# Ordering GpSimd's operator work by VectorE's reads, and next states ahead of the GELU's transposes, in the S5 stages of a hybrid trunk

## The chip, the cores and the metric

The kernel runs on one core of one Trainium2 chip. The metric is the device time of one execution in microseconds. Three runs of the kernel before took 2251.64, 2251.73 and 2249.75 us, the median is 2251.64 us. The core has TensorE (PE in the profile, with its weight loads as PEld), VectorE (DVE), ScalarE (ACT), GpSimd (POOL) and SyncE (SP, which here only issues transfers).

## The reference

The model is a trunk of four layers over a sequence of 512 rows and 1024 columns in float32. The mixers are S5, gated linear attention, differential attention, and S5 again; each is followed by a SwiGLU network with 2816 hidden columns. The change lies in the two S5 mixers. Cut to what matters, one of them computes:

```python
ab = exp(lam * dt)                      # complex, 64 groups x 64 states
bb = (ab - 1) / lam * b                 # 64 groups x 64 states x 16 inputs
u  = rmsnorm(x, g)                      # 512 x (64 groups x 16 inputs)
s[t] = ab * s[t-1] + bb @ u[t]          # per group: a complex scan over time
y[t] = real(c @ s[t]) + d * u[t]
z  = gelu(y)
a, b = split(z @ w_glu, 2)              # 1024 x 2048
x  = x + a * sigmoid(b)
```

## The kernel before, in words

**Tiling.** The 64 groups are worked in eight rounds kk of eight groups, four pairs of two groups b in each; a pair's two times 64 complex states fill the 128 partitions. Time is folded: 512 rows are 128 steps m of four rows each, so that a state advances by the fourth power of ab per step. For each round there are small operators: `in` (two 128x512 tiles, from X), `out` (from Q), `map` (the direct path of the four rows onto one another, from X, Q and d), `cs` (cosine and sine of the phase at each m) and `r4` (the decay per step).

**The pipe.** `s5_pipe` does both S5 stages. Its parts for round kk are:

- `up_first`, `up`: TensorE transposes the input of the round (`up` tile), ScalarE (in the second S5's first four rounds VectorE) copies it to `room`.
- `products` (L1588): 8 TensorE products of `room` with `in` into the two PSUM banks `V`.
- `states` (L1593 to L1598): six VectorE operations 128x512; the first four read `V` from PSUM and `cs`, the last two add in SBUF. The results are in `mods` (m[:, 0] and m[:, 2]; m[:, 2] is written last).
- `scan` (L1602): two VectorE scans over m, both inputs in SBUF.
- `turn` (L1611, L1615): four VectorE products that turn the states back into `prods` (q), both inputs in SBUF.
- `outputs` (L1622, L1624): for each pair b one TensorE product of `room` with `map` and four of `prods` with `out`, all into the PSUM tile `y`; then ScalarE's GELU (L1626).
- `turned` (L1642, L1643): four TensorE transposes of the GELU's output into the PSUM tile `zp`, and ScalarE's rounded copy of it into `zT`; `rest` (L1647): VectorE's remainder of the rounding, the second half of `zT`.
- `glu`: twelve TensorE products per round (L448 to L450) of `zT` with the rounded weights and their remainder into four accumulators. Each product comes in three parts: high by high, high by low, low by high.

The tiles `up`, `xps`, `y`, `zp`, `rps` and `cps` share two PSUM banks (tag "tp"); `rough`, `angle` and the GLU's accumulators share four (tag "acc").

**The order of the work.** Within the pipe the order on every engine and queue is the order in which the code issues it (`hand_all`): nothing is moved by the planner there. Ahead of the pipe, `hand` fixes TensorE's and ScalarE's order only, and behind the pipe the planner of the framework orders the work by its own costs. In round kk the loop issues the states of kk, the outputs of kk-1, the transposes `up` of kk+2, `turned(kk-1)`, `products(kk+1)`, the scans and turns of kk, `rest(kk-1)` and `glu(kk-2)`. Hooks put a stage's own work between these.

**The first S5's own work.** `s5_first` makes the operators inside the pipe, for groups of two rounds h = 0 to 3. `s5_x` makes X[h] in three parts: `pre` (the gain's product L1264, then six operations of 128 columns, L1239 to L1241), `one` and `two` (three operations of 384 columns each). h = 0 is VectorE's, the others are GpSimd's. `s5_q` makes Q[h] on VectorE (six operations of 512 columns in the odd rounds), from a product and a ScalarE copy in the even round before. `ins` transposes X on TensorE (`xps`) and ScalarE copies it into `in` (L1409). `rows` multiplies X's and Q's first parts (`rps`, L1352), and `s5_map` combines them on VectorE and ScalarE, writes them to DRAM (`rd`, L1368, SP's queue) and reads them back as `map` by four transfers on SP's queue and four on GpSimd's (L1377). The phases are made by `rough` and `angle` products on TensorE out of `counts` and `frow`, with ScalarE's roundings, VectorE's `clip` (L1212, a PSUM read) and ScalarE's sines. Tables for the sine and the GELU are loaded anew by ScalarE when it goes from one to the other (1.28 us each).

Before the change, `new_x(1)` is issued ahead of the pipe and runs on GpSimd from 22.4 us; `new_x(2)` and `new_x(3)` are issued whole behind the turns of rounds 1 and 3. No semaphore other than the data's own holds them back.

**The second S5** reads its operators from DRAM, where the first layer's network has spilled them; it has no operator work in the pipe.

## Time and profile before

| what | us |
|---|---|
| median of three runs | 2251.64 |
| the profiled execution | 2249.67 |
| its span | 2248.0 |
| TensorE busy | 2174.6 (97%) |
| VectorE busy | 1635.6 (73%) |
| ScalarE busy | 1138.7 (51%) |
| GpSimd busy | 341.1 (15%) |
| first S5's states, round 0 to round 7 | 31.2 to 125.6 |
| second S5's states, round 0 to round 7 | 1746.9 to 1815.8 |

A row of the timeline has the start, the length, the engine, the line of the kernel, the operation, what it writes and reads, the shape, and how many it merges; in brackets stands how long the engine was idle before and who released it. A row of the waits has the engine, the waiting tile and line, the releaser, the total, the times and the longest. A row of the chain has start, length, engine, tile and line. A row of a source line has the shortest, the median and the longest duration in ns. The end of a VectorE operation overlaps the start of the next by some 0.08 us, so operations of 0.68 us stand 0.60 us apart.

### The profile page before, as it was taken

To read this page: it belongs to the slowest core of one execution; us is meant where nothing else is said; L and a number is where in the kernel's file an instruction comes from. 1 tells how busy PE (TensorE), PEld (TensorE's weight loads), DVE (VectorE), ACT (ScalarE), POOL (GpSimd) and SP (SyncE) were. 2 spreads that over 40 slices of the span, in tenths; PEclk is the share of its full clock that TensorE was granted. 3 is DMA by queue.
4 is the path that set the end of the run, shared out by engine and by line. 5 is a ranking of instruction groups with operands and counts; after the bars stand their busy time and mean duration, and the time that the engine had idled before them with its cause. 6 is when DMAs were issued, how large, how long until landed. Compare 5 with 4: busy or idle time off the path is not lost.

```text
span 2248.0 us, 38450 instructions
## 1 busy us (share of the span) xinstructions
PE 2174.6 (97%) x15415; PEld 1971.6 (88%) x15415; DVE 1635.6 (73%) x2495; ACT 1138.7 (51%) x1827; POOL 341.1 (15%) x447
## 2 busy tenths in 40 slices
PE   6999999999999999999999999999999899999998
PEld 5888979989988899999888888999998888989997
DVE  9955868786878598776745676967766965957675
ACT  8534635444655365564435776644544234635443
POOL 5401141431211010100002221110000001101000
PEclk9999999999999999999999999999999999999999
DMA  4356666674863666765337465985631546766622
GB/s 90 65 171 169 164 159 174 174 184 131 206 152 95 168 168 191 179 171 139 104 128 160 96 148 141 243 207 136 184 94 47 160 141 159 196 160 164 165 76 75
DMA packets 309180, 333.62 MB, mean 148 GB/s; under 512 B 70477, under 2 KB 253033, under 8 KB 308874
## 3 DMA queue, kind: packets, MB, share of 16 engines
q1 hardware_dynamic: 238970, 238.93, 35.0%
q0 software_dynamic: 70032, 92.23, 21.9%
q8 instruction: 121, 1.98, 0.4%
q14 instruction: 57, 0.47, 0.1%
HBM read 297.16 MB, written 18.75 MB: 141 GB/s over the span
## 4 chain that ended last, share of the span: by engine, by line
PE 81%; DVE 8%; ACT 4%; issue 3%; DMA 1%; SPq 1%; POOL 0%; DVEq 0%; POOLq 0%; ACTq 0%
PE a L594 20%; PE acc L448 11%; PE acc L450 11%; PE acc L449 11%; PE c L594 10%; PE d L594 5%; PE y L1624 2%; DVE whl L428 2%; ACT whl L420 1%; PE op L2590 1%; PE V L1588 1%; PE s L2557 1%; PE tp L117 1%; PE acc L2645 1%; DMA wst<-in_ffn_w_down_dram 1%
## 5 line engine op out<-in xcount | busy, mean ns | idle before, releaser
L428 DVE TENSOR_TENSOR whl<-wst,whl 128x1024 fp32r<-128x1024 f32 x260 | 316.8, 1223 | 224.5 <-ACT whl L420 223.4
L420 ACT CAST whl<-wst 128x1024 fp32r<-128x1024 f32 x260 | 272.1, 1051 | 256.3 <-PE acc L450 164.6
L594 PE MATMUL a<-side,whl 128*128 128x256 f32 x3240 | 392.5, 277 | 6.7 <-DVE whl L428 6.3
L594 PEld LDWEIGHTS a<-side,whl 128*128 128x128 f32 x3240 | 379.0, 188 | 9.0 <-DVE whl L428 7.3
L448 PE MATMUL acc<-whl,act 128*128 128x512 f32 x704 | 276.2, 393 | 0.9 <-DVE g L768 0.9
L449 PE MATMUL acc<-whl,act 128*128 128x512 f32 x704 | 274.9, 391 | 0.0
L450 PE MATMUL acc<-whl,act 128*128 128x512 f32 x704 | 274.8, 390 | 0.0
L594 PE MATMUL c<-side,whl 128*128 128x256 f32 x2160 | 261.3, 277 | 3.5 <-DVE whl L428 3.5
L594 PEld LDWEIGHTS c<-side,whl 128*128 128x128 f32 x2160 | 253.0, 188 | 4.4 <-DVE whl L428 4.3
L428 DVE TENSOR_TENSOR whl<-slot,whl 128x1024 fp32r<-128x1024 f32 x105 | 127.6, 1221 | 60.7 <-ACT whl L420 60.7
L448 PEld LDWEIGHTS acc<-whl,act 128*128 128x128 f32 x704 | 132.4, 188 | 29.6 <-DVE g L768 1.5
L450 PEld LDWEIGHTS acc<-whl,act 128*128 128x128 f32 x704 | 132.4, 188 | 27.7
L449 PEld LDWEIGHTS acc<-whl,act 128*128 128x128 f32 x704 | 132.5, 188 | 26.4 <-issue 0.2
L420 ACT CAST whl<-slot 128x1024 fp32r<-128x1024 f32 x105 | 109.9, 1053 | 86.3 <-PE acc L450 46.3
L594 PE MATMUL d<-sides,whl 128*128 128x256 f32 x1080 | 132.3, 278 | 2.5 <-ACT whl L420 2.5
L594 PE MATMUL a<-sides,whl 128*128 128x256 f32 x1080 | 132.6, 279 | 1.6 <-DVE whl L428 1.2
L594 PEld LDWEIGHTS d<-sides,whl 128*128 128x128 f32 x1080 | 127.9, 188 | 3.3 <-ACT whl L420 3.3
L594 PEld LDWEIGHTS a<-sides,whl 128*128 128x128 f32 x1080 | 128.2, 188 | 2.8 <-DVE whl L428 1.4
L428 DVE TENSOR_TENSOR whl<-halves,whl 128x1024 fp32r<-128x1024 f32 x87 | 105.8, 1221 | 30.7 <-ACT whl L420 30.4
L420 ACT CAST whl<-halves 128x1024 fp32r<-128x1024 f32 x87 | 91.0, 1051 | 70.6 <-DVE halves L817 26.0
L759 POOL DMA_DIRECT2D wst<-in_ffn_w_gate_up_dram x44 | 57.2, 1299 | 448.7 <-DMA wst<-in_ffn_w_gate_up_dram 144.5
L865 ACT CAST act<-r 128x512 fp32r<-128x512 f32 (+1 forms) x110 | 66.1, 642 | 106.0 <-DVE r L846 85.4
(496 smaller groups left out, 4068.6 us busy)
## 6 DMA issues: line engine op xcount, KB each, us to landing
wst<-in_ffn_w_gate_up_dram SPq DMA_DIRECT2D x88, 512.0 KB, 4.6
wst<-in_ffn_w_down_dram SPq DMA_DIRECT2D x88, 512.0 KB, 4.6
slot<-in_ffn_w_gate_up_dram SPq DMA_DIRECT2D x69, 512.0 KB, 6.2
wst<-in_ffn_w_gate_up_dram POOLq DMA_DIRECT2D x44, 512.0 KB, 6.1
halves<-in_ffn_w_gate_up_dram SPq DMA_DIRECT2D x42, 512.0 KB, 6.5
wst<-in_s_w_glu_dram SPq DMA_DIRECT2D x32, 512.0 KB, 4.9
wst<-in_diff_w_qkv_dram SPq DMA_DIRECT2D x24, 512.0 KB, 4.4
slot<-in_ffn_w_gate_up_dram POOLq DMA_DIRECT2D x18, 512.0 KB, 9.2
```

What stands on the lines that cost most here:

```text
L117: tr.nc.tensor.transpose(p[:, j], h[:, j * P : (j + 1) * P], tr.ident[:])
L420: self.last["high"] = self.nc.scalar.copy(hl[:, 0], w[:])
L428: self.last["low"] = self.nc.vector.tensor_tensor(hl[:, 1], w[:], hl[:, 0].bitcast(F32), op=ALU.subtract)
L448: mm(out, lh, rh, start=first, stop=False)
L449: mm(out, lh, rl, start=False, stop=False)
L450: self.last["mm"] = mm(out, ll, rh, start=False, stop=last)
L594: mm(o, *two, start=first and not (j or k or n), stop=k == 3 and n == 2, skip_group_check=True,)
L759: nc.gpsimd.dma_start(w[:], left.quarter(*plus, b), accum_op=ALU.add)
L865: self.last["act high"] = nc.scalar.copy(dst[:, 0, j], src[:, j])
L1588: mm(V[kk][z][:, bs(b)], inm[:, z, bs(b)], U[:, bs(b)], start=True, stop=True)
L1624: mm(yb[:, b], q[:, j, b], om[:, j // 2, bs(b)], start=False, stop=j == 3)
L2557: nc.tensor.matmul(ss[m][:], qs[:, m, ts], ks[:, m, z], start=z == 0, stop=z == 1)
```

## The change

- The two `counts` tiles are made by eight ScalarE multiplications of 128x128 instead of two VectorE products of 128x512.
- The two halves of `mops` are zeroed elsewhere: `mops[0]` by GpSimd ahead of the pipe, `mops[1]` by ScalarE at the end of round 0 (before: both by ScalarE ahead of the pipe).
- GpSimd's work on X[1] to X[3] is issued in single parts, and ahead of each part GpSimd copies one column from a tile that VectorE writes into the last column of X, so that it waits for that VectorE operation. Behind Q[h]'s last operation (`behind_q`) go: `pre` of X[1], `pre` of X[2], `one` of X[3]. Behind the states (`turned_in`) go: `one` of X[1] (round 0), `one` of X[2] (round 2), `pre` of X[3] (round 3), `two` of X[3] (round 4). Behind the second turn (`turned_out`) go: `two` of X[1] (round 0), `two` of X[2] (round 2). The parts behind the states of rounds 0, 2 and 4 stand in GpSimd's queue ahead of that round's map transfers.
- In round 1 the clips of the phases 4 and 5 come behind `rest(0)` instead of ahead of it.
- In both S5 stages `products(kk+1)` is issued ahead of `turned(kk-1)`, and in rounds 3 to 8 the first products of `glu(kk-2)` ahead of that: two in rounds 3 to 5 of the first S5 and none in those of the second, four in rounds 6 to 8 of both. The order of the GLU's twelve products within a round is changed so that these need no low part of the weights.
- In `outputs(0)` the four products with `map` are issued together: behind the sixteen with `out` in the first S5, ahead of them in the second.

```diff
-            v.tensor_tensor(
-                self.counts[:, z], y.unsqueeze(2).broadcast_to([P, 4, P]),
-                self.mrow[:].unsqueeze(1).broadcast_to([P, 4, P]), op=ALU.mult,
-            )
+            for j in range(4):
+                nc.scalar.mul(self.counts[:, z, j], self.mrow[:], y[:, j : j + 1])
...
+        self.turned_in = lambda kk: hold[kk % 2][0][:, 2, 511:]
+        self.turned_out = lambda kk: hold[kk % 2][1][:, 1, 3, 127:]
...
-            for b in range(4):
+            if kk == 0:
+                by_map = [(b, U[:, bs(b)], mop[:, bs(b)]) for b in range(4)]
+                by_state = [(b, q[:, j, b], om[:, j // 2, bs(b)]) for b in range(4) for j in range(4)]
+                whole = by_map + by_state if left else by_state + by_map
+                for n, (b, x, y) in enumerate(whole):
+                    mm(yb[:, b], x, y, start=n == 0, stop=n == 19, skip_group_check=True)
+            for b in range(4 if kk else 0):
...
-        def glu(kk):
+        order = {}
+
+        def glu(kk, n=12):
...
+            if kk not in order:
+                split = [(t, n) for t in range(2) for n in (0, 2)] + [(0, 1), (1, 1)] if 0 < kk < KT - 1 else []
+                order[kk] = split + [(t, n) for t in range(len(split) // 3, NT) for n in range(3)]
             hl = hls[kk // 2]
...
+            for t, m in order[kk][:n]:
+                mm(
+                    accs[t][:], zT[:, m // 2, kk, t * P : (t + 1) * P], hl[:, m % 2, kk % 2],
+                    start=kk == 0 and m == 0, stop=kk == KT - 1 and m == 2,
                 )
+            del order[kk][:n]
...
                 hook("ahead of zp", kk)
+                if 3 <= kk < 9:
+                    glu(kk - 2, 4 if kk > 5 else 0 if left else 2)
+                if kk + 1 < 8:
+                    products(kk + 1)
                 if 1 <= kk < 9:
                     turned(kk - 1)
                 hook("behind zp", kk)
                 if kk == 8:
                     glu(6)
-                if kk + 1 < 8:
-                    products(kk + 1)
                 hook("behind products", kk)
...
+            def new_x(h, n=0, behind=None):
+
+                if n == 0:
+                    X[h] = self.s5_x(nc.gpsimd if h else nc.vector, p, 0, 8 * h, 8, raw[h][0], 2, gain)
+                if behind is not None:
+                    last = X[h][0][:, 1, 7, 3, 15:]
+                    nc.gpsimd.tensor_copy(last, behind)
+                X[h][1 + n]()
...
-                self.zero_off(mops[z].unsqueeze(1), 64, nc.scalar)
+            self.zero_off(mops[0].unsqueeze(1), 64, nc.gpsimd)
...
-                with self.tc.issue_after(self.last_pow.ins):
-                    new_x(1)
...
+                new_x(1, 0, behind_q(0))
+
+            def behind_q(h):
+                return Q[h][0][:, 1, 7, 4, 15:]
...
             def ahead_of_low(kk):
                 h = kk // 2
+                for at, x, n in ((0, 1, 1), (2, 2, 1), (3, 3, 0), (4, 3, 2)):
+                    if kk == at:
+                        new_x(x, n, self.turned_in(kk))
                 if kk in (2, 4, 6):
                     self.s5_map(0, 8 * h, 8, rv[h], rs, mops[h % 2])
...
-                if kk in (1, 3):
-                    new_x(kk // 2 + 2)
+                if kk in (0, 2):
+                    new_x(kk // 2 + 1, 2, self.turned_out(kk))
...
+            def last(kk):
+                if kk == 0:
+                    self.zero_off(mops[1].unsqueeze(1), 64, nc.scalar)
                 if kk == 1:
                     phases((4, "clip"), (5, "clip"))
+                if kk in (1, 3):
+                    new_x(kk // 2 + 2, kk // 2, behind_q(kk // 2 + 1))
```

10 lines of the change are left out of this document (1 added, 9 removed).

## The prediction, made before the result was known

> **What bounds the kernel now.** I read the page first, then the busy time by stretch, the waits of TensorE by stretch, and last the chain and the timeline of the two S5 stages.
>
> ```profile
> span 2248.0 us, 38450 instructions
> PE 2174.6 (97%) x15415; PEld 1971.6 (88%) x15415; DVE 1635.6 (73%) x2495; ACT 1138.7 (51%) x1827; POOL 341.1 (15%) x447
> ```
>
> TensorE (PE) is busy for 97% of the span, so a change is worth what it takes from TensorE's waits, and it can cost what it adds to them. The edits lie in the first S5 stage (0 to 143 us) and the second (1741 to 1836 us).
>
> ```profile
> 36.00:60.00 24.00, 18.99 (x181) 16.46 (x181) 23.93 (x33) 18.82 (x34) 15.04 (x19) 0.93 0.34 64
> 85.00:97.90 12.90, 12.21 (x153) 10.92 (x151) 12.90 (x18) 6.70 (x11) 9.71 (x13) 1.00 0.29 60
> 1776.00:1836.00 60.00, 56.83 (x409) 52.05 (x409) 51.11 (x71) 17.83 (x28) 0.32 (x3) 1.00 0.46 133
> ```
>
> Columns: length, then busy time of PE, weight load, VectorE (DVE), ScalarE (ACT), GpSimd (POOL), then the granted clock. Rounds 0 and 1 of the first S5 (36 to 60) are VectorE's: it is busy 23.93 of 24 us while TensorE idles 5 us and is granted 0.93 of its clock. From round 2 on, both are nearly full: in round 4 (85 to 97.9) VectorE 12.90 and TensorE 12.21 of 12.90. In the second S5 TensorE leads.
>
> The waits of TensorE from 60 to 143 us, then from 1776 to 1836 us (total, times, longest):
>
> ```profile
> PE zp L1642 <- ACT inm L1409: 2.5, 4, 0.7
> PE y L1622 <- DVE zT L1647: 1.1, 1, 1.1
> PE zp L1642 <- ACT gain L1626: 0.7, 1, 0.7
> PE zp L1642 <- ACT z L1626: 0.7, 1, 0.7
> PE V L1588 <- ACT inm L1409: 0.7, 1, 0.7
> ```
>
> ```profile
> PE zp L1642 <- ACT room L1626: 3.2, 6, 0.7
> ```
>
> So from 60 us on the first S5 offers 5.7 us at most, and the second 3.2 us, nearly all of it where the transposes zp of the GELU's output stand in TensorE's queue and wait for ScalarE.
>
> **The second S5: next states ahead of the transposes.** In each round TensorE now issues `products(kk+1)` before `turned(kk-1)`, and in rounds 6 to 8 four GLU matmuls before both. The matmul pitch:
>
> ```profile
> 1821.55 0.40 PE L449 MATMUL acc<-whl,zT 128*128 128x512 f32 x1
> 1821.78 0.39 PE L450 MATMUL acc<-whl,zT 128*128 128x512 f32 x1
> ```
>
> is 0.23 us, so four are 0.92 us and cover a 0.75 us GELU wait; in rounds 3 to 5 products(kk+1) (some 2 us) cover 0.31 us each. All six waits go: -3.2 us. What is late next: zp and ScalarE's copy of it come up to 2 us later in a round, and VectorE's `rest` behind them; in this stretch no wait of TensorE is put down to VectorE, so I cost that at nothing; if VectorE had no time in hand, the gain would be 0. Rounds 0 to 2, where the map products now precede the state products of round 0, run behind VectorE's turns, and I count no gain there. Ends 0 to -4, taken -3.2, nearest to the row of waits.
>
> **The start of the first S5.** VectorE loses two row-count products like the one below (1.35 us together); ScalarE gains eight copies 128x128 and gives back four zeroing copies of 64x512; GpSimd gains two memsets of 64x512 while it idles.
>
> ```profile
> L1165 DVE TENSOR_TENSOR counts<-ident,mrow x1: 673/673/673, 7.5 to 7.5; 128x512 fp32r<-128x512 f32 x1
> 18.94 3.63 PE warmed L1342 x24
> 23.04 0.57 ACT frow L1183
> 30.57 0.61 ACT cs L1217
> 40.63 1.20 DVE prods L1615 x2
> ```
>
> The last four lines are of the chain. From 18.94 us it runs over TensorE's warming matmuls and ScalarE's copies and sines to the first states at 31.2 us, not over VectorE. So I take 0 for the counts (no row has a 128x128 copy on ScalarE; eight at up to 0.59, the 64x512 copy's row below, less four given back, add at most 2.4 us, of which ScalarE's waits hold most; ends -0.4 to +0.8).
>
> **What a GpSimd instruction costs VectorE.**
>
> ```profile
> L1239 DVE TENSOR_TENSOR Q<-Q,pw x8: 675/886/1324, 25.1 to 108.0; 128x512 f32<-128x512 f32 x8
> L1239 POOL TENSOR_TENSOR X<-X,pw x6: 840/1288/1292, 27.9 to 88.3; 128x384 f32<-128x384 f32 x6
> 51.74 0.89 DVE L1239 TENSOR_TENSOR Q<-Q,pw 128x512 f32<-128x512 f32 x1
> 84.71 0.40 POOL L1240 TENSOR_TENSOR dx<-bb,s5fi 128x128 f32<-128x128 f32 x1
> 85.60 0.68 DVE L1594 TENSOR_TENSOR mods<-V,cs 128x512 f32<-128x512 f32 x1
> 85.61 0.85 POOL L1239 TENSOR_TENSOR X<-X,pw 128x384 f32<-128x384 f32 x1
> L1602 DVE TENSOR_TENSOR_SCAN mods<-r,mods x16: 1187/1201/2012, 36.5 to 127.2; 128x512 f32<-128x512 f32 x16
> 90.93 1.86 POOL L1241 TENSOR_TENSOR X<-X,dx 128x384 f32<-128x384 f32 x1
> 91.85 3.13 DVE L1602 TENSOR_TENSOR_SCAN mods<-r,mods 128x512 f32<-128x512 f32 x2
> 78.86 2.59 POOL L1264 TENSOR_TENSOR bb<-bb,gain 128x256 f32<-128x256 f32 x1
> ```
>
> The same VectorE product takes 0.675 us alone, 0.89 beside 128-column GpSimd work (+0.21) and 1.324 beside 384 columns (+0.65). Beside a PSUM read (85.60) neither loses: 0.68 and 0.85. A pair of scans takes 3.13 us instead of 2 x 1.19 when it meets a GpSimd instruction: +0.75. So the scans to which the change ties groups are no free place, and PSUM reads are. I price a 384-column instruction in scans, turns or `low` at 0.65, a 128-column one at 0.21, the gain product at 0.45.
>
> [...]
>
> **Rounds 0 and 1.**
>
> ```profile
> 34.21 1.51 DVE L1598 TENSOR_TENSOR mods<-mods 128x512 f32<-128x512 f32 x1
> 40.19 2.37 POOL L1377 DMA_DIRECT2D scr<-rd x4 [3.21 <-DMA rd<-rsb]
> 44.91 0.76 PE L1622 MATMUL y<-scr,room 128*128 128x128 f32 x2 [2.92 <-DMA scr<-rd]
> 51.01 0.60 ACT L1626 ACTIVATE gain<-y 128x512 f32<-128x512 f32 x1 [0.95 <-PE y L1624]
> 53.51 1.17 ACT L1409 COPY inm<-xps 64x512 f32<-64x512 f32 x2 [1.90 <-PE xps L1386]
> 55.23 1.95 PE L1588 MATMUL V<-room,inm 128*128 128x128 f32 x16
> 60.07 0.49 PE L1622 MATMUL y<-scr,room 128*128 128x128 f32 x2 [1.11 <-DVE zT L1647]
> ```
>
> Round 0: X[1]'s first part, now behind Q[0], lies beside the states' PSUM reads and frees 0.83 us (1.51 to 0.68); its second part meets the clip (PSUM) once and the scans twice, +1.3; its third part stands in GpSimd's queue behind the four map transfers and falls into states(1): 0. (The transfers are issued from 40.19 to 42.56 and landed by 44.9, so 2.3 us after the last issue.) The turns end at 41.83 + 0.5 = 42.3. The state products of outputs(0) start then and the map's four come last, so the 2.92 us wait for the map's transfers goes, and the slow clock after it. But ScalarE has the two zeroing copies of mops[1] more (2 x 0.59) ahead of the GELU, and had 0.95 to spare: GELU(0) at 51.3 instead of 51.01. From there: 51.9, the copies of inm 1.17 to 53.1, products(2) 1.95 to 55.05, zp 0.66 and the rough matmuls to 56.6, rps 0.7 to 57.3. VectorE's rest(0) now comes ahead of two clips and ends at 56.8. So outputs(1) starts near 57.3 instead of 60.07: -2.8 us. The cover that decides here is ScalarE.
>
> **Rounds 2 to 9.**
>
> ```profile
> 59.94 0.67 DVE L1593 TENSOR_TENSOR mods<-V,cs 128x512 f32<-128x512 f32 x1
> 71.37 0.67 DVE L1593 TENSOR_TENSOR mods<-V,cs 128x512 f32<-128x512 f32 x1
> 86.93 0.69 PE L1352 MATMUL rps<-Q,bpad 128*32 128x64 f32 x32
> 97.88 0.67 DVE L1593 TENSOR_TENSOR mods<-V,cs 128x512 f32<-128x512 f32 x1
> 109.33 0.69 DVE L1241 TENSOR_TENSOR Q<-Q,dq 128x512 f32<-128x512 f32 x1
> ```
>
> VectorE's states(2) start behind the clips at 56.8 + 1.2 = 58.0 (59.94 before). Round 2 takes 71.37 - 59.94 = 11.43 us, in which GpSimd met only PSUM reads. Now X[2]'s second part adds 3 x 0.65 = 1.95 in `low` and the scans, the third one collision with a turn, 0.65 (the rest meets `rest`, a clip and states): states(3) at 58.0 + 11.43 + 2.6 = 72.0, over at 75.6 (six products at the 0.6 us pitch of 85.60). Round 3 up to the end of Q, taken from the undisturbed round 5, is 110.0 - 97.88 = 12.1 us, and X[3]'s first part, tied to the scans, meets scans, turns and Q with all seven instructions: 0.45 + 6 x 0.21 = 1.7. Q[2] ends at 72.0 + 12.1 + 1.7 = 85.8. TensorE, nearly 3 us ahead, must wait there for rps, which started at 86.93: **-1.1 us** is what is left of rounds 0 and 1.
>
> Behind it VectorE is lighter than before (round 4 loses X[3]'s first and most of its second part), so TensorE leads again, and keeps the filled waits: two GLU matmuls 0.46 in rounds 4 and 5 each, 0.4 in round 6, 0.75 in rounds 7 and 8: 2.8 us. The third part of X[3] stands in GpSimd's queue ahead of round 4's map transfers, which then land about when outputs(4) needs them: +0.5. First S5: -1.1 - 2.8 + 0.5 = -3.4 us (ends: +1 to -5.8, the rivals).
>
> **The sum.** -3.4 - 3.2 + 0 = -6.6 us. The profiled execution took 2249.67 us around its span of 2248.0, so 2243.1; it stands 1.97 below the median of the three runs (2251.64; 2249.75 to 2251.73). Against that median I go half way: 2244 us.
>
> **The rivals.**
> *GpSimd's groups are nearly free.* If GpSimd waits for PSUM reads more than it holds scans up, Q[2] is no limit and the first S5 keeps 2.8 + 0.46 (round 3) + 2.8 = 6.1. With 3.2: -9.3, about 2241.5. For it: the groups behind Q meet only PSUM reads. Against: the 3.13 row.
>
> *Each collision costs the whole GpSimd instruction* (0.84 and 0.40 rows). Round 2 then adds 4 x 0.84 = 3.4, round 3 some 0.6 + 6 x 0.4 = 3.0; Q[2] ends at 87.9, +1.0 over before instead of -1.1. The first S5 comes to 1.0 - 2.8 + 0.5 = -1.3, the sum -4.5: 2246, at the edge of no change. With less to win in the second S5 it lands inside. [...]
>
> *Slower: GpSimd's queue.* Between states(3) (75.6 us) and round 4's map transfers stand 13 instructions of X[3]. If each starves as the gain product did at 78.86 (2.59 us), they end at 109.3, the transfers' 2.1 us of issue and 2.3 of landing follow, and outputs(4) start at 113.7 instead of 100.9: +12.8 - 2.4 - 3.2 = +7 us, about 2259. It decides from some 2.4 us an instruction; the 0.84 to 1.86 of the other rows speak against it.
>
> Also, the planner may order the work outside the hand-ordered stretches anew; the rows give it no sign, and it widens both sides.
>
> **How the numbers follow.** 0.2% (4.5 us) is about what a measurement of this kernel can tell from no change. The forecast 0.45 (faster), nearly free groups 0.17 (faster), whole collisions 0.25 (same), the queue or the planner 0.13 (slower). Faster 0.62, same 0.25, slower 0.13. The range 2238.5 to 2253 takes in the free groups and the whole collisions with the planner's spread on both; the forecast's own is 2241 to 2247.
>
> **What would show it.** Right: in the second S5 no wait of zp on the GELU; no wait for the map's DMA near 44 us; zp behind V; scans of 1.8 to 2.0 us in rounds 0, 2, 3 and 4; rps of round 4 waiting for Q; outputs(0) at the full clock. Wrong: scans at 1.2 us beside GpSimd's groups (gain near 9), TensorE waiting for `scr<-rd` in rounds 2 and 4, for X before xps, or for VectorE's turns in the second S5.

## The result, and the profile after

The changed kernel took 2248.72 us, the median of 17 runs (2245.63 to 2252.70, leaving out one run far off all others, as there was one of the kernel before too), beside 2252.17 us for the kernel before in runs on the same chip. The ratio is 0.9985, with a 95% interval of 0.9977 to 0.9993. A second measurement (the last experiment) gave 0.9991, 0.9981 to 1.0000. So by medians the change is worth 2.4 to 3.5 us. The first interval lies clear of 1, the second touches it, and both gains stay inside the 0.2% that the prediction took as the limit of what can be told: a small gain, a third to a half of the forecast 6.6 us. The time lies within the range that was given (2238.5 to 2253), which was wide enough to hold the time without any change as well, and outside the forecast's own 2241 to 2247.

The profiled execution took 2246.31 us around a span of 2244.6, 3.4 us less than that of before. Its span and busy times:

```profile
span 2244.6 us, 38453 instructions
PE 2176.7 (97%) x15415; PEld 1972.1 (88%) x15415; DVE 1634.8 (73%) x2493; ACT 1139.4 (51%) x1833; POOL 344.1 (15%) x458
```

The busy time of the stretches that the prediction showed (length, then PE, weight load, VectorE, ScalarE, GpSimd, then the granted clock):

```profile
36.00:60.00 24.00, 18.19 (x146) 15.74 (x146) 22.10 (x28) 17.59 (x31) 17.68 (x26) 0.86 0.28 58
85.00:97.90 12.90, 12.41 (x141) 10.82 (x141) 12.83 (x17) 4.64 (x8) 11.86 (x16) 1.00 0.15 34
1776.00:1836.00 60.00, 60.00 (x432) 55.48 (x431) 52.36 (x74) 18.99 (x29) 0.31 (x3) 1.00 0.50 146
```

The second S5 (last line) did what was forecast: TensorE is busy for all 60 us, where it was busy for 56.83. Rounds 0 and 1 of the first S5 (first line) did not: TensorE is busy for 18.19 us where it was 18.99, at a clock of 0.86 where it was 0.93, and now VectorE idles as well (22.10 of 24). The waits of TensorE say why, first from 36 to 60 us, then from 60 to 150 us (total, times, longest):

```profile
PE y L1626 <- DMA scr<-rd: 4.4, 1, 4.4
```

```profile
PE V L1588 <- ACT inm L1407: 1.3, 4, 0.7
PE acc L448 <- ACT gate L2047: 1.2, 1, 1.2
PE y L1628 <- DMA bpad<-X: 1.1, 1, 1.1
```

The wait of outputs(0) for the map's transfers did not go, it grew from 2.92 to 4.37 us. Two smaller ones are new: outputs(4) for round 4's map (1.1; the view names another transfer that landed there, but in experiment 6, with the map's transfers issued first, the wait is gone), and the gate, which stands in ScalarE's queue behind a weight cast that waits for its own transfer (1.2).

To see where the time went I set the start of every TensorE product against that of the same product before (both kernels have 15415 in nearly the same order). The difference is +3.0 us at 53 us, +1.8 at 160.8 us, where the first S5 is over; -0.4 at 1740.8 us, +0.9 at 1775.3 us and -3.4 at 1832.9 us. The step from +1.8 to -0.4 lies in stages that the change doesn't touch. It is the clock, in the stretch 285 to 300 us, of before, of the changed kernel, and of the changed kernel profiled a second time:

```profile
285.00:300.00 15.00, 12.10 (x91) 9.00 (x90) 12.39 (x42) 6.79 (x21) 7.78 (x11) 0.89 0.63 157
```

```profile
285.00:300.00 15.00, 13.18 (x102) 10.23 (x101) 13.45 (x42) 6.84 (x22) 7.48 (x10) 1.00 0.69 180
```

```profile
285.00:300.00 15.00, 14.66 (x105) 11.38 (x104) 13.45 (x42) 6.83 (x22) 7.47 (x10) 0.94 0.69 175
```

The clock column reads 0.89, 1.00 and 0.94: it differs between two executions of the changed kernel as well. In the profile of experiment 3, whose clock fell at the same place as before's (293.5 us), the difference does not move there. (In between it moves by up to 2 us and back, at other stretches at half clock.) The step to +0.9 is the clock too: the record of the granted clock has one stretch at half clock near 1750 us in before and two in the changed kernel, and one again in its second profile, where the difference does not move between 1740.8 and 1775.3 us. So the two S5 stages are read by themselves below, each from its own start to its own end: "the first S5's balance" is the difference at product 1200 (160.8 us in before), "the second's" that between products 12300 and 12700 (1775.3 to 1832.9 us in before). For the changed kernel they are **+1.8** (forecast -3.4) and **-4.3** (forecast -3.2).

### The profile page after: what moved, and what is told of

It reads as the page before. It is cut to its first block, busy times and chain, and to the rows that moved or that the text cites. A ratio compares the mean times of both kernels' runs of the same rounds, so it can differ in the third digit from the quotient of the medians.

```text
span 2244.6 us, 38453 instructions
## 1 busy us (share of the span) xinstructions
PE 2176.7 (97%) x15415; PEld 1972.1 (88%) x15415; DVE 1634.8 (73%) x2493; ACT 1139.4 (51%) x1833; POOL 344.1 (15%) x458
## 4 chain that ended last, share of the span: by engine, by line
PE 79%; DVE 8%; issue 4%; ACT 4%; DMA 3%; POOL 1%; SPq 1%; DVEq 0%; POOLq 0%; ACTq 0%
PE a L594 19%; PE acc L448 11%; PE acc L450 11%; PE acc L449 11%; PE c L594 10%; PE d L594 5%; DVE whl L428 2%; PE y L1630 2%; ACT whl L420 1%; PE acc L1666 1%; PE op L2620 1%; PE s L2587 1%; PE tp L117 1%; PE V L1588 1%; PE acc L2675 1%
## 5 line engine op out<-in xcount | busy, mean ns | idle before, releaser
L428 DVE TENSOR_TENSOR whl<-wst,whl 128x1024 fp32r<-128x1024 f32 x260 | 317.0, 1224 | 222.4 <-ACT whl L420 221.6
L428 DVE TENSOR_TENSOR whl<-slot,whl 128x1024 fp32r<-128x1024 f32 x105 | 127.8, 1222 | 60.6 <-ACT whl L420 60.6
L428 DVE TENSOR_TENSOR whl<-halves,whl 128x1024 fp32r<-128x1024 f32 x87 | 105.9, 1223 | 32.9 <-ACT whl L420 32.6
L420 ACT CAST whl<-halves 128x1024 fp32r<-128x1024 f32 x87 | 91.0, 1051 | 72.5 <-DVE halves L817 25.8
```

Of the source, the lines that this page charges most:

```text
L420: self.last["high"] = self.nc.scalar.copy(hl[:, 0], w[:])
L428: self.last["low"] = self.nc.vector.tensor_tensor(hl[:, 1], w[:], hl[:, 0].bitcast(F32), op=ALU.subtract)
```

## What the late group looks like

The first part of X[1] on GpSimd in the changed kernel, then the ScalarE copy ahead of it, then TensorE's outputs(0) and outputs(1) (start, duration, engine, line; in brackets the idle time before it and what ended it):

```profile
37.27 0.10 POOL L1224 MEMSET r<- 128x4 f32 x1 [4.56 <-DMA craw<-in_s_c_im_dram]
37.31 1.08 POOL L1794 COPY X<-Q 128x1 f32<-128x1 f32 x1
38.36 0.72 POOL L1262 TENSOR_TENSOR bb<-bb,gain 128x256 f32<-128x256 f32 x1
...
42.81 0.46 POOL L1239 TENSOR_TENSOR X<-X,dx 128x128 f32<-128x128 f32 x1
43.20 0.19 POOL L1794 COPY X<-mods 128x1 f32<-128x1 f32 x1
...
46.37 2.38 POOL L1375 DMA_DIRECT2D scr<-rd  x4
```

```profile
36.61 0.60 ACT L1223 COPY r<-s5r 128x512 f32<-128x512 f32 x1
```

```profile
42.32 3.84 PE L1626 MATMUL y<-scr,prods 128*128 128x128 f32 x32
50.53 2.04 PE L1626 MATMUL y<-scr,room 128*128 128x128 f32 x8 [4.37 <-DMA scr<-rd]
...
61.69 0.49 PE L1628 MATMUL y<-scr,room 128*128 128x128 f32 x2
```

The group is issued behind `decays(1)`. That step has a small memset on GpSimd (L1224) which must follow ScalarE's copy of the same tile (L1223), and the copy is done only at 37.2 us. (The view puts the memset's wait down to a transfer; the kernel has the copy ahead of it, and in experiment 3 the same memset, at 36.77 us, is put down to `ACT r L1223`.) X[1]'s first part follows that memset in the order of issue on GpSimd's queue, and in the trace its first instruction starts at 37.31 us, behind the memset at 37.27; the part lasts until 43.3 us, where the prediction had it beside the first states at 31.2. X[1]'s second part follows, then the map's four transfers, at 46.37 instead of 40.19 us; they have landed at 50.5. outputs(0) starts its state products at 42.32, as forecast (42.3), and then waits 4.37 us for the map.

## The experiments

All times are medians; ratios are against the kernel before in the same session, with their 95% intervals.

**1. TensorE's order alone.** The kernel before with the new order of TensorE's work and nothing else.

```diff
+            if kk == 0:
+                by_map = [(b, U[:, bs(b)], mop[:, bs(b)]) for b in range(4)]
+                by_state = [(b, q[:, j, b], om[:, j // 2, bs(b)]) for b in range(4) for j in range(4)]
+                whole = by_map + by_state if left else by_state + by_map
...
+                if 3 <= kk < 9:
+                    glu(kk - 2, 4 if kk > 5 else 0 if left else 2)
+                if kk + 1 < 8:
+                    products(kk + 1)
                 if 1 <= kk < 9:
                     turned(kk - 1)
...
-                if kk + 1 < 8:
-                    products(kk + 1)
```

> The kernel before with TensorE's order alone changed (products(kk+1) and the first GLU products ahead of the transposes, outputs(0) with its map products together); counts, zeroing, GpSimd's groups and the clips as before. Theory (GpSimd's queue made the first S5 lose its share): the second S5 gains 3.0 us as in the changed kernel, the first S5 gains 2.5 to 3.5 us (filled waits of rounds 3 to 8; outputs(1) stays at 60 us because VectorE's Q and clips of round 1 still stand ahead of rest(0)); total -5.5 to -6.5 us. Rival (the new order on TensorE itself costs the first S5): first S5 +1 to +2, total -1 to -2.

Measured: 2245.82 us, ratio 0.9977 (0.9967 to 0.9987). The first S5's balance is -0.7, the second has no wait left. Order alone is faster than the whole change. The map's wait at outputs(0) is gone: without X[1]'s group ahead of them the transfers are in time. What stands in the first S5 after that:

```profile
PE rps L1352 <- DVE Q L1241: 1.6, 2, 1.1
PE up L1567 <- ACT gain L1632: 1.6, 1, 1.6
```

The wait of rps for Q[2] is the limit that the prediction named. The gain in the first S5 is smaller than the 2.5 to 3.5 us expected. Part of the time taken from the GELU's waits comes back at Q[2]; the first states also came 0.7 us later in this execution, and 3.41 us at half clock follow the wait at `up`, so the shares are not parted.

**2. The operator work alone.** The kernel before with all the rest: GpSimd's groups, counts, zeroing; TensorE in its old order.

```diff
+                new_x(1, 0, behind_q(0))
...
+                for at, x, n in ((0, 1, 1), (2, 2, 1), (3, 3, 0), (4, 3, 2)):
+                    if kk == at:
+                        new_x(x, n, self.turned_in(kk))
...
+                if kk in (0, 2):
+                    new_x(kk // 2 + 1, 2, self.turned_out(kk))
```

> The kernel before with all of the first S5's edits off TensorE (counts by ScalarE, zeroing, GpSimd's groups, clips behind rest), TensorE's order as before. Theory: the map of round 0 lands near 50.5 us and TensorE waits for it at the head of outputs(0), 7 to 8 us; first S5 +4 to +5 us, second S5 0, total +4 to +5. Rival (TensorE's order costs the first S5): first S5 at or below 0.

Measured: 2255.98 us, ratio 1.0022 (1.0014 to 1.0031): slower. The first S5's balance is +4.8, the second's 0. One wait holds it, that of outputs(0) for the map:

```profile
PE y L1622 <- DMA scr<-rd: 8.4, 1, 8.4
```

Here the map's products come first in outputs(0), so all of the late transfers shows at once, 8.4 us where the changed kernel hides half of them behind the state products. The pair parts the change in two: the order brings 5.4 us by medians, the rest with the groups as placed costs 4.8. Together they come out better than their sum, since the new order of outputs(0) hides part of what the groups delay.

**3. X[1]'s first part ahead of the memsets.** The changed kernel with one line moved, so that the group is issued ahead of `decays(0)` and `decays(1)`.

```diff
                 rows[1]()
+                new_x(1, 0, behind_q(0))
                 decays(0)
...
                 raw[2] = self.s5_loads(p, 0, 16, 8, 2)
-                new_x(1, 0, behind_q(0))
```

> The changed kernel with X[1]'s first part issued ahead of the memsets of the decays of rounds 0 and 1 on GpSimd's queue, nothing else. Theory: it runs from 29 to 34 us, the second part follows the states of round 0, the map transfers are issued near 40.5 instead of 46.4 us, the 4.4 us wait for scr<-rd near 46 us and the slow clock behind it go, and the first S5 comes out 3 to 5 us shorter than in the changed kernel, total -6 to -8 against the kernel before. Rival (collisions with VectorE set the first S5): wait gone, first S5 within 1 us of the changed kernel's.

Measured: 2242.15 us, ratio 0.9958 (0.9945 to 0.9972), some 6 us below the changed kernel by medians. Part of that is the clock: three of its five runs had a granted clock of 0.998, the changed kernel's 0.993 to 0.996, and its two others took 2246.06 us (0.995) and 2248.5 (0.994). The group runs at 29.4 us, beside the first states, and the map's wait is gone. In the profiled execution, which was this kernel's slowest run (2248.5), the balance of the first S5 is only -0.1, 2 us better than the changed kernel and not the 3 to 5 expected, because another wait stands next and the clock falls behind it (it is 0.50 from 52 to 56 us):

```profile
52.10 1.11 PE L1567 MATMUL up<-ident,scr 128*128 128x128 f32 x4 [2.88 <-ACT gain L1632]
```

**4. No operator work for the later rounds.** As the changed kernel, but X[1], X[2] and X[3] are not formed: all rounds use X[0], so the input operators of rounds 2 to 7 are left out of the computation.

```diff
             def new_x(h, n=0, behind=None):
+                if h:
+                    X[h] = X[0]
+                    return
```

> The changed kernel without GpSimd's work on X[1] to X[3] (X[0] is used in their place, so the operators of rounds 2 to 7 are left out and the output is not the reference's). It shows what all of GpSimd's arithmetic, its collisions with VectorE (9.3 us of lengthened VectorE operations in the changed kernel) and its place ahead of the map transfers cost together. Theory: VectorE's rounds shorten by the collisions, TensorE leads from round 2 on; the first S5 is 7 to 10 us shorter than in the changed kernel. Rival (TensorE's order is the limit): at most 2 us shorter.

Measured: 2242.70 us, ratio 0.9957 (0.9944 to 0.9969). First S5's balance -2.2. That is 4.0 us better than the changed kernel, not the 7 to 10 expected. Against experiment 3 the medians are the same, but at different clocks (0.994 to 0.996 here). The two profiles compare better: they meet the same wait of 2.9 us at 49 us with 6.83 us at half clock behind it, and the balances differ by 2.1 us. So in these profiles GpSimd's arithmetic for three operators, with its collisions and the wait for round 4's map behind it, costs some 2 us of the first S5 once the first group is moved.

**5 and 6. What stands next: ScalarE's zeroing, and round 4's map.** Both build on experiment 3. Number 5 zeroes the second map on GpSimd at the start instead of on ScalarE in round 0; number 6 puts the map's transfers of rounds 2, 4 and 6 ahead of the group on GpSimd's queue.

```diff
-            self.zero_off(mops[0].unsqueeze(1), 64, nc.gpsimd)
+            for z in range(2):
+                self.zero_off(mops[z].unsqueeze(1), 64, nc.gpsimd)
...
-                if kk == 0:
-                    self.zero_off(mops[1].unsqueeze(1), 64, nc.scalar)
```

> The kernel with X[1]'s first part put ahead of round 0's decay memsets left TensorE waiting 2.88 us at 49.2 us for GELU(0), whose predecessor on ScalarE includes the second map buffer's zeroing, two copies of 1.25 us in all at 46.22. Here that zeroing is done by GpSimd at the start of the stage and ScalarE has none of it in round 0. Theory: ScalarE's queue sets that wait; GELU(0) begins 1.25 us sooner, the wait shrinks to about 1.6 us, and the first S5 is 1.0 to 1.3 us shorter than there: about 2241 us, ratio to the kernel before near 0.9953. Rival: GELU(0)'s place is set by the third block's sines or the table load alone, or the next wait takes over; then the wait keeps 2.5 us or more and the time stays at 2242.

```diff
+                if kk in (2, 4, 6):
+                    self.s5_map(0, 8 * h, 8, rv[h], rs, mops[h % 2])
                 for at, x, n in ((0, 1, 1), (2, 2, 1), (3, 3, 0), (4, 3, 2)):
                     if kk == at:
                         new_x(x, n, self.turned_in(kk))
-                if kk in (2, 4, 6):
-                    self.s5_map(0, 8 * h, 8, rv[h], rs, mops[h % 2])
```

> X[1]'s first part ahead of round 0's decay memsets as there, and in rounds 2 and 4 (and 6) the four map transfers stand on GpSimd's queue ahead of the operator group instead of behind it. Theory: round 4's transfers are issued at about 91.5 instead of 96.9 us, round 2's at 66.3 instead of 69.6, so the wait of 1.17 us of outputs(4) for the map at 101.5 goes and nothing replaces it; the first S5 is 0.8 to 1.2 us shorter than with the group first, about 2241 us. The groups then start 2 us later and may miss the scans they were tied to, with no cost beyond 0.5 us. Rival: the transfer's own path is late (it lands as late as before), or the operators of the following rounds come late by the 2 us: no change, or a wait of about 1 us at the next row products.

Number 5: 2246.11 us, ratio 0.9982 (0.9973 to 0.9992); the wait at `up` kept 2.55 us, so the theory falls: ScalarE's queue is not what is late there (more in 8). The time is 4 us over number 3's median, which the rival did not have either. The start came 0.9 us later than number 3's; with the same start code as number 8, whose first states came at 30.96 us against 31.98 here, the start varies by a microsecond by itself. From its own start the first S5 is as long as number 3's within 0.3 us (balances +0.5 and -0.1), one more sign that number 3's low median is in part the clock.

Number 6: 2243.75 us, ratio 0.9968 (0.9956 to 0.9981). The wait for round 4's map went, as expected, and a wait of 1.47 us for Q[2] took its place; the first S5's balance is -2.85. This is the cleanest view of what the prediction had worked out (TensorE, then VectorE's first operation of states(2) and states(3)):

```profile
57.34 0.49 PE L1628 MATMUL y<-scr,room 128*128 128x128 f32 x2
85.59 0.68 PE L1350 MATMUL rps<-Q,bpad 128*32 128x64 f32 x30 [1.47 <-DVE Q L1239]
58.38 0.68 DVE L1593 TENSOR_TENSOR mods<-V,cs 128x512 f32<-128x512 f32 x1
70.17 0.68 DVE L1593 TENSOR_TENSOR mods<-V,cs 128x512 f32<-128x512 f32 x1
```

Of the 2.7 us between the balances of 3 and 6, 2.1 are there by 60 us and are the clock again: both go on at `up` at 52.10 us. The granted clock (the number behind the five busy times) from 48 to 60 us, of experiment 3 and then of 6:

```profile
48.00:52.00 4.00, 1.22 (x33) 1.01 (x32) 4.00 (x6) 3.82 (x7) 0.11 (x1) 0.89 0.01 3
52.00:56.00 4.00, 3.90 (x17) 3.56 (x18) 3.93 (x8) 1.68 (x4) 0.00 (x0) 0.50 0.00 0
56.00:60.00 4.00, 4.00 (x50) 3.43 (x49) 2.23 (x4) 2.14 (x4) 2.97 (x8) 0.76 0.35 70
```

```profile
48.00:52.00 4.00, 1.76 (x35) 1.21 (x34) 4.00 (x6) 3.83 (x7) 0.11 (x1) 1.00 0.03 10
52.00:56.00 4.00, 3.50 (x27) 3.18 (x28) 3.93 (x8) 2.00 (x5) 0.00 (x0) 1.00 0.00 0
56.00:60.00 4.00, 4.00 (x58) 3.45 (x57) 4.00 (x7) 3.94 (x7) 2.97 (x8) 1.00 0.35 70
```

**7. The counts undone.** Both mends of 5 and 6 together (which is number 8), with the row counts by VectorE as before the change.

```diff
-            for j in range(4):
-                nc.scalar.mul(self.counts[:, z, j], self.mrow[:], y[:, j : j + 1])
+            v.tensor_tensor(
+                self.counts[:, z], y.unsqueeze(2).broadcast_to([P, 4, P]),
+                self.mrow[:].unsqueeze(1).broadcast_to([P, 4, P]), op=ALU.mult,
+            )
```

> The same as the kernel with both mends (zeroing at the start, maps first), but the row counts are formed by VectorE in two products again instead of by ScalarE in eight copies: this undoes the one part of the change that only the start shows. The prediction held this part for nothing, since the first states wait for ScalarE's sines and not for VectorE: states(0) begins within 0.4 us of the other kernel's and the time is the same within 1 us. Rival: ScalarE is what the start waits for, so its eight copies of 0.34 us (2.7 us) delay the first states: then states(0) begins 1 to 2.5 us sooner here and the time is shorter by as much.

Measured: 2243.95 us, ratio 0.9968 (0.9955 to 0.9980), against 2244.66 for number 8. The rival falls: the start was not sooner but 1.4 us later than number 8's at product 100, which is not much more than the microsecond by which the start varies (see 5). The theory's 0.4 us for the first states is missed by the same microsecond. The counts cost nothing that can be measured.

**8. Both mends together:** the edits of 5 and 6 on top of 3, with the counts on ScalarE as in the change.

> Both mends together on top of X[1]'s first part ahead of round 0's decay memsets: the second map's zeroing by GpSimd at the start, and the map transfers ahead of the groups. If both theories hold the gains add, since one lies in round 0 and the other in round 4: about 2240 us, ratio near 0.995, first S5 about 2.3 us shorter than before the change. If one wait only hides the next (the cast of the GLU weights waited for its transfer at 145 us by 1.2 to 1.7 us in every kernel so far, and grows when the stage gets shorter), half of it comes: about 2241 us.

Measured: 2244.66 us, ratio 0.9972 (0.9961 to 0.9983); balance -2.8, as in 6 alone, so the two gains did not add: the zeroing had none to give. The wait at `up` is still 2.58 us with the zeroing away. ScalarE now stands idle ahead of the third block's sines:

```profile
48.06 0.63 ACT L1213 ACTIVATE cs<-cs 128x512 f32<-128x512 f32 x1 [1.35 <-DVE cs L1210]
```

So what GELU(0) waits for is VectorE: its clip of the third block (L1210, 47.35 us) stands behind all of states(1), the sines behind the clip, and the GELU behind the sines.

**9. That clip ahead of states(1).** On top of 6.

```diff
             def behind_states(kk):
-                if kk == 1:
-                    phases((3, "clip"), (3, "sines"))
...
             def last(kk):
                 if kk == 0:
+                    phases((3, "clip"), (3, "sines"))
                     self.zero_off(mops[1].unsqueeze(1), 64, nc.scalar)
```

> The kernel with X[1]'s first part early and the map transfers first, and the third block's clip and sines moved from behind states(1) to the end of round 0, ahead of states(1). GELU(0) waited there behind those sines (48.1 to 50.0 us) and TensorE waited 2.34 to 2.58 us at 'up' for it. GELU(0) now begins by about 48 us and that wait goes. Theory: VectorE runs without a gap from 35 to 64 us and sets rounds 1 to 4, so the wait was free: outputs(1) comes up to 2 us sooner, but rps of round 4 stays at 85 to 86 us behind Q[2] and the whole is within 0.5 us of the 2243.7 measured without the move. Rival: TensorE's wait was on the path and outputs(1), states(3) and rps of round 4 all come 2 us sooner: about 2241.5 us.

Measured: 2242.31 us, ratio 0.9964 (0.9951 to 0.9978). The premise failed: GELU(0) did not come sooner. ScalarE had no idle time left, and the zeroing filled what the clip had freed:

```profile
49.13 1.23 ACT L1320 COPY scr<-ident 64x512 f32<-64x512 f32 x2
50.38 0.62 ACT L1223 COPY r<-s5r 128x512 f32<-128x512 f32 x1
51.02 1.28 ACT L1632 ACT_TABLE_LOAD   x1
52.31 0.60 ACT L1632 ACTIVATE gain<-y 128x512 f32<-128x512 f32 x1
```

So the run tells nothing of whether that wait (2.05 us here) is on the path. Its balance is -0.9, not better than 6: it started 1.1 us later, and 3.41 us at half clock follow the wait.

**10. Only the transfers ahead.** The changed kernel with X[1]'s first part where it is, and the map's transfers of rounds 0, 2, 4 and 6 ahead of the second part (or the group).

```diff
-                    self.s5_map(0, 0, 8, rv[0], rs, mops[0])
...
+                if kk in (0, 2, 4, 6):
+                    self.s5_map(0, 8 * h, 8, rv[h], rs, mops[h % 2])
                 for at, x, n in ((0, 1, 1), (2, 2, 1), (3, 3, 0), (4, 3, 2)):
```

> The changed kernel with X[1]'s first part left where it is, behind the decay memset of round 1 on GpSimd's queue, but round 0's four map transfers put ahead of X[1]'s second part on that queue, and those of rounds 2, 4 and 6 ahead of their groups. This parts the two costs of the late X[1]: the transfers queued behind it, and its collisions with turns(0) and states(1). Theory: the wait of 4.37 us for the map is nearly all of the loss of round 0; the transfers are issued at about 41.5 us at the latest instead of 46.37, the wait falls below 1 us, outputs(1) is at 57 to 58.5 us instead of 61.69 and the first S5 is 3 to 4.5 us shorter than in the changed kernel: about 2244.5 us. Rival: the collisions with turns(0) and states(1) matter themselves; then outputs(1) is at 60 us or later though the map is there, and the time stays over 2246.5.

Measured: 2246.14 us, ratio 0.9977 (0.9968 to 0.9986); balance +0.35, 1.1 to 1.4 us better than the changed kernel's two profiles. Less than the 3 to 4.5 expected: the first part alone, behind the memset, holds GpSimd until 42.75 us, and the map has landed only at 49.4:

```profile
42.75 2.38 POOL L1375 DMA_DIRECT2D scr<-rd  x4
49.39 2.04 PE L1626 MATMUL y<-scr,room 128*128 128x128 f32 x8 [3.70 <-issue]
```

The wait is still 3.70 us, and behind it the eight products take 2.04 us (half clock) instead of the 1.13 of experiment 6; outputs(1) is at 60.62 us. The slowest of the map's transfers took 4.5 us from issue to landing, where the changed kernel's took 2.7 at most. A weight transfer of 512 KB was issued on SP's queue at 44.29 us, just ahead of the last of them; whether it held them up was not tried. With the first part moved as well (experiment 6) the transfers are issued from 41.32 us and the wait is 0.42. So the place of the first part, not of the second, is what has to be mended; experiment 3 does that.

**11. Clip and zeroing together:** the edit of 9 on top of 6, and the zeroing as in 5.

```diff
                 if kk == 0:
-                    self.zero_off(mops[1].unsqueeze(1), 64, nc.scalar)
+                    phases((3, "clip"), (3, "sines"))
```

> The kernel with X[1]'s first part early, the map transfers first, the third block's clip and sines ahead of states(1), and now the second map's zeroing by GpSimd at the start as well. Each of the last two alone left GELU(0) where it was: with the zeroing gone ScalarE waited 1.35 us for the clip, with the clip early the zeroing of 1.23 us filled the gap. Together they leave neither, so GELU(0) begins 1.2 us sooner after states(0) than in either, and the wait at 'up' falls from 2.1 to about 0.9 us. Theory, VectorE sets rounds 1 to 4 (no gap in it from 35 to 56 us): the wait for Q[2] at rps of round 4 grows by as much as 'up' shrinks, rps goes on 53.8 us after the first states (85.65 less 31.16 in the kernel without the two, 54.5), and the time is within 0.7 us of 2243. Rival, the wait was on the path: rps of round 4 comes 1.2 us sooner or more after states(0), about 53.2 us, and the time is about 2242 or less.

Measured: 2243.83 us, ratio 0.9968 (0.9958 to 0.9978). Now GELU(0) does come sooner, and the wait at `up` is down to 0.77 us. A wait for Q[1] at the next rps is new, and that for Q[2] at rps of round 4 stays:

```profile
51.06 0.65 PE L1567 MATMUL up<-ident,scr 128*128 128x128 f32 x4 [0.77 <-ACT gain L1632]
56.58 0.68 PE L1350 MATMUL rps<-Q,bpad 128*32 128x64 f32 x30 [0.82 <-DVE Q L1239]
85.44 0.69 PE L1350 MATMUL rps<-Q,bpad 128*32 128x64 f32 x30 [1.48 <-DVE Q L1239]
```

rps goes on 53.9 us after the first states (85.44 less 31.56), where it was 54.5 in number 6 (85.59 less 31.10): as the theory had it (53.8; the rival 53.2), and the time is that of 6 and 8. Of 1.6 us of wait taken away 0.8 came back at once and 0.6 was left at round 4: most of the wait at `up` had been free, because VectorE sets these rounds. (These are single executions.)

**12. The changed kernel again,** with no edit, beside number 11 in one session.

> The changed kernel itself, timed beside the mended one on the same chip, so that the two can be set against each other: 2248.7 us by its first measurement, that is 4 to 6 us more than the mended kernels. A second profile shows which of its waits are of the program: theory: the wait of 4.4 us for round 0's map, of 1.1 us for round 4's and of 1.2 us for the gate's cast come again within 0.3 us, and the half-clock windows behind 100 us stand elsewhere than in the first profile. Rival: the waits themselves move from one execution to the next.

Measured: 2248.41 us, ratio 0.9991 (0.9981 to 1.0000), 4.6 us over number 11. Its waits came again:

```profile
PE y L1626 <- DMA scr<-rd: 4.7, 1, 4.7
```

for round 0's map, 1.1 for round 4's, 1.3 for the gate's cast. The first S5's balance is +1.4 (+1.8 in the first profile), the second's -4.3 in both. The waits belong to the program; the clock behind 285 us doesn't.

The versions of experiments 3, 6, 9 and 11 all beat the kernel before, by 7 to 9 us, and by medians the changed one by 4 us or more; in the profiles the first S5 is 2 us shorter than the changed kernel's in number 3 and 4 to 5 in numbers 6 and 11. Their intervals overlap, so none is called the best; number 3 needs the move of one line.

## Why the prediction was half right

| | forecast | changed kernel | experiment 6 |
|---|---|---|---|
| state products of outputs(0) | 42.3 us | 42.32 | 41.81 |
| GELU(0) | 51.3 | 52.61 | 51.45 |
| outputs(1) | 57.3 | 61.69 | 57.34 |
| states(2) | 58.0 | 62.66 | 58.38 |
| states(3) | 72.0 | 75.52 | 70.17 |
| Q[2] ready, rps of round 4 | 85.8 | 88.46 | 85.59, waiting for Q |
| first S5's balance | -3.4 | +1.8, +1.4 | -2.85 |
| second S5's balance | -3.2 | -4.3, -4.3 | -4.3 |

**The step that failed** is the first sentence on round 0: "X[1]'s first part, now behind Q[0], lies beside the states' PSUM reads and frees 0.83 us". The working looked at what the group waits for by its own operand (Q[0], ready by then), and not at what stands ahead of it on GpSimd's queue: the memsets of `decays(0)` and `decays(1)`, each behind a ScalarE copy. A row of before would have told it, the second memset's wait for that copy:

```profile
36.88 0.11 POOL L1226 MEMSET r<- 128x4 f32 x1 [1.66 <-ACT r L1225]
```

From it follows the rest: X[1] 6 us late, the transfers behind X[1] 6.2 us late, and the step "the 2.92 us wait for the map's transfers goes, and the slow clock after it", which turned into a wait of 4.37 us and a slow clock behind it. Experiment 3 moves that group alone and the map's wait goes; experiment 2 shows its price with the old order of outputs(0); with it and the maps in place (6) the working from GELU(0) on comes out within 0.4 us at every point but states(3), which is 1.8 us sooner, since the groups then start behind the transfers and meet the turns and states(3) instead of the scans. Two of these agreements are luck. Q[2] comes at 85.59 because two errors cancel: round 2 took 11.8 us where 14.0 had been worked out, round 3 15.4 where 13.8 had been. And the changed kernel's 42.32 comes out though the scans of round 0 met nothing (2.34 us the pair; 1.3 had been counted): the first part, late, lengthened the turns by 0.7 instead, and the first states were 0.4 later.

**A second step had no term:** with the map's wait the working took the slow clock as gone. In the mended kernels TensorE waits 0.8 to 2.9 us for GELU(0) at `up` instead, and with that the clock fell in four of the seven. The first S5's balance is -2.85, -2.8 and -3.4 in experiments 6, 8 and 11, where it stays up, and -0.1, +0.5, -0.3 and -0.9 in 3, 5, 7 and 9, where 3.41 or 6.83 us at half clock follow (5, 7 and 9 also started 0.9 to 1.3 us later). So the forecast -3.4 is reached where the clock happens to hold.

**The queue rival** named the right engine and queue, in the wrong round: it put the slow instructions ahead of round 4's map and asked for 2.4 us each. Apart from the gain product (below) they took 0.4 to 1.8 us, and round 4's map was late by 1.1 us (forecast +0.5, mis-sized since the three products before the transfers took 1.75 to 1.82 us each beside the scans, not 0.84). Number 6 shows that term as 0 with the transfers first.

**The price of a collision in the scans was right, their number was not.** The scans of rounds 2 and 4, against round 2's of before:

```profile
64.95 2.33 DVE L1602 TENSOR_TENSOR_SCAN mods<-r,mods 128x512 f32<-128x512 f32 x2
```

```profile
67.67 3.59 DVE L1602 TENSOR_TENSOR_SCAN mods<-r,mods 128x512 f32<-128x512 f32 x2
95.00 3.58 DVE L1602 TENSOR_TENSOR_SCAN mods<-r,mods 128x512 f32<-128x512 f32 x2
```

are 1.26 us longer a pair, 0.63 for a scan, where 0.65 for an instruction was taken. But three GpSimd products ran there, from 66.54 to 72.06 us, and beside the scans' 1.26 us they cost VectorE only 0.2: `low` (L428) took 1.23 us against 1.21 before, and the last product ended beside a clip (0.66 us as before) and the first turn (0.84 against 0.67). Round 2's third part met nothing (0.65 had been counted), since it came out behind the map's transfers, and the scans of rounds 0 and 3 met nothing either. So round 2 grew by 1.4 us, from 11.43 to 12.86, where 2.6 had been worked out, and round 3 took 13.0 where 13.8 had been; from states(2) to the first rps of round 4 the changed kernel takes 25.8 us, and 27.8 had been worked out.

The rival of whole collisions asked for 3.4 us in round 2 and 3.0 in round 3, so it was not what halved the gain. A whole collision is 0.84 us, what such a GpSimd product takes beside VectorE's PSUM reads (0.84 at 89.89 and at 90.69 us); here each scan lost 0.63 us, and the three products took 1.75 to 1.92. The rival of nearly free groups fares better than it looks: experiment 4, with no groups at all, gained 8.5 us by medians against its -9.3. But that is not this kernel, in which the scans of rounds 2 and 4 were held up as priced and the place of one group decided.

**The second S5 was right in kind and too small by 1.1 us.** All six waits went. They sum to 3.2 us, and the shift is 4.3: it goes in three steps of 0.5 us and three of 0.9, each some 0.2 us more than the wait that it takes away. In the rows of the prediction a product overlaps the one behind which it runs (0.40 us long at a pitch of 0.23). The author's estimate from these two numbers is that a wait taken out is worth its length and that overlap, some 0.17 us. That fits the steps; no run shows it by itself. The rounds "0 to 2" hold two more small waits of zp (0.9 us in all) in before and none after; by their own products they gave nothing, as forecast: the shift is the same at 1740.8 and at 1775.3 us in the second profile.

**The start** was right: 0 forecast; the first states came at 31.59 and 31.19 us in the two profiles, 31.21 before.

**The sum.** First S5 +1.4 to +1.8, second -4.3: some -2.7, which agrees with the measured -3.45 and -2.35. The forecast's -6.6 would have come out at -7.2 with the group in its place, and 2243.75 less 2251.14, experiment 6's -7.4, is that. So two errors lay on opposite sides, one of +5 and one of -1, and the range held the time because it was wide.

## What to carry to other kernels

To place work on a queue, look first at what stands ahead of it there and at what each of those instructions waits for: here a group behind a memset of 0.1 us, which follows another engine's copy, came 6 us late, and so did the transfers behind the group (6.2). Issue transfers that someone waits for ahead of arithmetic that is merely to be done in time. When a change moves the time by a few microseconds, compare stage by stage, since untouched stages shift by 2 us from one execution to the next. And see what TensorE will wait for next when a wait is taken away: here it was GELU(0), for 0.8 to 2.9 us, and in four of the seven mended kernels 3.41 or 6.83 us at half clock came behind it.

## What the runs showed of the hardware

**The clock was halved for 3.41 us or twice that, at some waits and not at others.** In the record of the granted clock of before and of the changed kernel, every stretch at one half but the one at the kernel's end lasts 3.41 or 6.83 us, and the stretches at full clock between them are multiples of 3.41 us as well (23.89, 245.76, 351.57, 1102.51 and 484.69 us in before). With the waits at 42 to 52 us it fell, in the wait or right behind it, at those of 2.9 us and more (2.88 in experiment 3, 2.9 in experiment 4, 2.92 in before, 3.70 in experiment 10, 4.37 and 4.65 in the changed kernel), but also at 1.60 and 2.05 us (experiments 1 and 9), and not at 2.34 and 2.58 us (experiments 6 and 8); with 2.55 us it stayed down for 6.83 us in experiment 5 and for 3.41 us in experiment 7. In these profiles a wait of 1.5 to 3 us was thus worth its length or some 2 us more, the author's estimate from one pair: 3 and 6 go on at `up` at the same time and are 2.1 us apart at 60 us. What decides whether the clock falls was not tried and stays open.

**Beside a run of VectorE's operations one GpSimd product took 4.22 us.** The gain product, which took 0.72 us for X[1] and for X[2] (at 38.36 and 58.43 us), met the turns of round 3 for X[3]:

```profile
81.38 4.22 POOL L1262 TENSOR_TENSOR bb<-bb,gain 128x256 f32<-128x256 f32 x1
```

```profile
81.94 0.68 DVE L1611 SCALAR_TENSOR_TENSOR prods<-mods,cs 128x508 f32<-128x508 f32 x1
82.54 1.28 DVE L1615 TENSOR_TENSOR prods<-mods,cs 128x508 f32<-128x508 f32 x2
83.73 0.69 DVE L1237 TENSOR_TENSOR Q<-Q,pw 128x512 f32<-128x512 f32 x1
```

VectorE's turns are within 0.01 us of those of round 2 of before (0.67 us, and 1.27 for two), and GpSimd's product lasts until 85.60 us; the first longer VectorE operation is L1239 at 85.06 (1.10 us). In experiment 6 the same product took 1.23 us in nearly the same place, a little later against VectorE's order. What makes the difference was not tried by itself and stays open.
